# Fewer unread products that keep TensorE's clock up, and a norm root moved from GpSimd to VectorE, in a four-layer hybrid model

## The chip, the cores and the metric

The kernel runs on one core of a Trainium2 chip. Five engines work side by side on a core: TensorE (PE in the profile, its weight loads PEld), VectorE (DVE), ScalarE (ACT), GpSimd (POOL) and SyncE (SP), which only issues transfers here. Each engine takes its instructions in the order in which the program gives them, and they wait for each other by semaphores. The metric is the device time of one execution in microseconds (us); the time of a kernel is the median of its runs.

## The reference, cut to what matters

The model has four layers over 512 tokens of 1024 features, all in float32. Each layer is a token mixer of another kind and a SwiGLU network with 2816 hidden features; all have a root-mean-square norm ahead of them.

```python
for i in range(DEPTH):                       # 4 layers
    hn = rmsnorm(h, norm_mix[i])
    m = (rwkv7_mix, swa_sink_mix, sgu_chunk_mix, gla_mix)[i](hn, ...)
    h = h + m
    h = h + swiglu(rmsnorm(h, norm_ffn[i]), ffn_w_in[i], ffn_w_out[i])
return rmsnorm(h, norm_final)
```

The change touches the first mixer. It has 16 heads of 64 features. For every token a 64x64 state of each head is decayed, corrected and read; the read rows are then normed head by head, and it is the root of that norm which the change moves:

```python
def step(state, inp):
    r_t, d_t, k_t, v_t, kk_t, a_t = inp
    sa = jnp.einsum('bhvk,bhk->bhv', state, kk_t)
    state = (state * d_t[:, :, None, :]
             - sa[..., None] * (kk_t * a_t)[:, :, None, :]
             + v_t[..., None] * k_t[:, :, None, :])
    return state, jnp.einsum('bhvk,bhk->bhv', state, r_t)
...
mean = jnp.mean(y, -1, keepdims=True)
var = jnp.mean(jnp.square(y - mean), -1, keepdims=True)
y = ((y - mean) * lax.rsqrt(var + RW_GN_EPS)).reshape(B, S, D) * gn_g + gn_b
bonus = (jnp.sum(hs(r) * hs(k) * r_k, -1, keepdims=True) * hs(v)).reshape(B, S, D)
return ((y + bonus).astype(x.dtype) * g) @ w_o
```

## The kernel before, in words

**Products.** A float32 weight tile (`wraw`) arrives by a transfer. ScalarE rounds it to a high part (`whi`), VectorE takes the difference (`wlo`), and TensorE makes three products of high and low parts (`mm3`). Nearly all of TensorE's time goes to these. Plain float32 products, which go through TensorE in several passes and are seen as two records each in the trace, are used for small matrices and transposes.

**The first mixer.** Projections of r, k and v come first. The recurrence is then taken in chunks of 64 tokens, in four groups of four heads, n = 0 to 3. `ahead(n)` works out all of a group that needs no state: `rwkv_prepare` (decays by a scan, scaled keys), `rwkv_products` (64x64 products of the chunks, masked into `pr` or `pa`), `rwkv_inverse` (the inverse of a triangular 64x64 matrix for each chunk: blocks of 16 by 15 dependent pairs of a multiplication and a reduction on VectorE in `et`, then two levels of doubling in which products of 64x64 on TensorE alternate with steps on ScalarE and VectorE in `mt`; the results are `iv`) and `rwkv_direct`. `rwkv_chain(n)` walks through the eight chunks with the state (`st`); each step goes from TensorE to ScalarE (`vu`) and back, and to VectorE (`st`) and back. After every half of the chain `rwkv_out` norms the rows (`out`), adds the bonus and gates them into `rk`. `ahead(n + 1)` is written ahead of `rwkv_chain(n)`, so the two can be mixed. For n = 0 the tiles of the inverse are called `slot`, and the projection of v is mixed in. Then `rwkv_out_proj` multiplies by the output weights (`et,rk`), the last two rows of weights follow as `whi,rk`, and the rest of the model follows.

**The order of the work.** All calls on engines are recorded as operations with their dependencies (`record`, L234 calls each later, so that this line stands for nearly all instructions in the profile). `price` gives each a cost by engine, operation and width. `run` then walks through the recorded operations like a list scheduler: at each step it takes the operation that can start first by its own clock of the engines, and emits it. So the order on every engine follows from the costs.

**Unread products.** `run` also keeps an account of TensorE's columns: `count` notes when each product runs and how many columns it streams, scaled by the rows in use. Two functions put in products of the identity with itself, which nobody reads (`product`, L478, `ps<-ident` in the profile). `keep_warm` fills the time in which TensorE waits for more than 450 ns by the account. `ahead_of_cold` puts a single one in front of an operation if fewer than `DENSE` columns ran in the last `TICK` (3.41 us). Each takes a bank of PSUM of its own from the pool of eight, and so may wait until the last reader of that bank is done. In the account TensorE runs at half speed in any tick after one with fewer than `BUSY` columns.

**The norm root.** `rwkv_out` sums the 64 values of each of 8 heads on VectorE (`gmean`, `gvar`). The scaling by 1/64, the addition of epsilon and three Newton steps of the inverse root (`rsqrt8`) are done on GpSimd in operations of 128x8, the first guess on VectorE. A second version, `rsqrt`, which works on VectorE alone with one guess and nine operations, is used elsewhere in the kernel.

## Time and profile before

| | |
|---|---|
| median of three runs | 2604.63 us (2602.24 to 2613.82) |
| the profiled execution | 2609.04 us, span 2607.3 us |
| mean granted clock of TensorE | 0.995 |
| PE busy | 2551.3 us, 98% of the span |
| DVE, ACT, POOL busy | 1795.0, 1313.8 and 368.2 us |
| L478, unread products | 524 records (262 products), 84.6 us busy |
| the first mixer's recurrence | about 189 to 520 us of the span |

A busy PE is not a PE that does useful work: the unread products count as busy. A group's row gives busy time and mean duration, then the idle time of its engine ahead of it and who ended it. A row of the windows view gives the stretch, its length, and for each engine the busy time and number of records inside it, then PEclk, the clock that was granted to TensorE (1.00 is full speed, 0.50 half), the share of the transfer engines that was busy, and GB/s. A row of the timeline gives start, length, engine, line, operation, tiles, shape and number of merged records, and in brackets an idle time ahead of it with its releaser.

### The profile page before, as it was taken

To read this page: it belongs to the slowest core of one execution; us is meant where nothing else is said; L and a number is where in the kernel's file an instruction comes from. 1 tells how busy PE (TensorE), PEld (TensorE's weight loads), DVE (VectorE), ACT (ScalarE), POOL (GpSimd) and SP (SyncE) were. 2 spreads that over 40 slices of the span, in tenths; PEclk is the share of its full clock that TensorE was granted. 3 is DMA by queue.
4 is the path that set the end of the run, shared out by engine and by line. 5 is a ranking of instruction groups with operands and counts; after the bars stand their busy time and mean duration, and the time that the engine had idled before them with its cause. 6 is when DMAs were issued, how large, how long until landed. Compare 5 with 4: busy or idle time off the path is not lost.

```text
span 2607.3 us, 37842 instructions
## 1 busy us (share of the span) xinstructions
PE 2551.3 (98%) x14518; PEld 2077.8 (80%) x14518; DVE 1795.0 (69%) x2801; ACT 1313.8 (50%) x2161; POOL 368.2 (14%) x517
## 2 busy tenths in 40 slices
PE   9999999999999999999999999999999999999998
PEld 8577777997878766978887888898877777888786
DVE  7675756478778864787777555487868634577868
ACT  4534453375546555655464333465555523565555
POOL 0000111112121332121211000022111000121111
PEclk9999999999999999999999999999999999999999
DMA  5210001378898432788995332399997221499985
GB/s 168 68 60 10 10 4 58 102 160 214 216 220 207 106 96 49 158 213 220 218 231 146 97 90 85 80 217 229 209 213 181 89 81 57 97 220 224 219 199 116
DMA packets 126581, 367.32 MB, mean 141 GB/s; under 512 B 13360, under 2 KB 20016, under 8 KB 126400
## 3 DMA queue, kind: packets, MB, share of 16 engines
q0 software_dynamic: 41472, 138.43, 29.8%
q1 hardware_dynamic: 84928, 226.47, 26.8%
q8 instruction: 114, 1.87, 0.3%
q14 instruction: 67, 0.55, 0.1%
HBM read 360.39 MB, written 2.10 MB: 139 GB/s over the span
## 4 chain that ended last, share of the span: by engine, by line
PE 49%; DMA 5%; DVE 4%; issue 4%; ACT 3%; POOL 1%; SPq 0%; DVEq 0%; POOLq 0%; ACTq 0%
PE ps L234 49%; DMA wraw<-ffn_w_b 2%; DVE slot L234 2%; DMA wraw<-ffn_o_a 2%; ACT slot L234 1%; DVE wlo L234 1%; ACT whi L234 1%; POOL wraw L234 1%; DMA wraw<-ffn_w_a 0%; DVE h L234 0%; DVE mx L234 0%; PE ps L478 0%; DMA wraw<-sg_w_v 0%; DMA slot<-slot 0%; DVE left L234 0%
## 5 line engine op out<-in xcount | busy, mean ns | idle before, releaser
L234 PE MATMUL ps<-whi,slot 128*128 128x512 f32 (+1 forms) x5072 | 1557.5, 384 | 17.6 <-DVE h L234 7.9
L234 PEld LDWEIGHTS ps<-whi,slot 128*128 128x128 f32 x5072 | 941.9, 188 | 201.2 <-issue 21.9
L234 DVE TENSOR_TENSOR wlo<-wraw,whi 128x1024 fp32r<-128x1024 f32 (+2 forms) x632 | 726.3, 1155 | 403.9 <-ACT whi L234 401.5
L234 ACT CAST whi<-wraw 128x1024 fp32r<-128x1024 f32 (+3 forms) x632 | 625.4, 993 | 731.3 <-PE ps L234 554.8
L234 PE MATMUL ps<-wlo,slot 128*128 128x512 f32 (+1 forms) x2536 | 967.5, 382 | 1.3 <-DVE wlo L234 1.2
L234 PEld LDWEIGHTS ps<-wlo,slot 128*128 128x128 f32 x2536 | 476.1, 188 | 85.5 <-DVE wlo L234 5.0
L234 PE MATMUL ps<-slot,whi 128*128 128x512 f32 (+2 forms) x864 | 275.1, 396 | 0.4 <-DVE slot L234 0.3
L234 DVE TENSOR_TENSOR slot<-ps,slot 128x512 f32<-128x512 f32 (+2 forms) x287 | 154.9, 566 | 68.5 <-PE ps L234 50.7
L234 PEld LDWEIGHTS ps<-slot,whi 128*128 128x128 f32 (+2 forms) x864 | 156.9, 184 | 49.0 <-DVE slot L234 6.9
L234 POOL DMA_DIRECT2D wraw<-ffn_w_a x128 | 109.4, 855 | 511.5 <-DVE wlo L234 399.6
L234 PE MATMUL ps<-slot,wlo 128*128 128x512 f32 (+2 forms) x432 | 169.5, 393 | 0.0
L234 POOL DMA_DIRECT2D wraw<-ffn_w_b x64 | 54.8, 865 | 766.3 <-DMA wraw<-ffn_w_b 494.1
L234 DVE TENSOR_TENSOR slot<-left,slot 128x512 fp32r<-128x512 f32 (+1 forms) x214 | 137.7, 662 | 34.8 <-ACT slot L234 29.3
L234 DVE TENSOR_TENSOR h<-h,ps 128x512 f32<-128x512 f32 x192 | 127.2, 683 | 30.4 <-PE ps L234 28.9
L234 ACT CAST slot<-left 128x512 fp32r<-128x512 f32 (+1 forms) x214 | 123.8, 599 | 32.9 <-PE ps L234 26.4
L234 ACT COPY slot<-ps 128x512 f32<-128x512 f32 (+1 forms) x138 | 75.7, 565 | 59.6 <-PE ps L234 53.3
L234 PEld LDWEIGHTS ps<-slot,wlo 128*128 128x128 f32 (+2 forms) x432 | 79.5, 184 | 20.2 <-issue 3.3
L234 POOL DMA_DIRECT2D wraw<-ffn_o_a x64 | 54.6, 854 | 275.8 <-DVE wlo L234 161.3
L234 PEld LDWEIGHTS ps<-ident,slot 128*128 128x128 f32 (+2 forms) x672 | 67.9, 139 | 29.3 <-issue 8.3
L234 PE MATMUL ps<-ident,slot 128*128 128x128 f32 (+2 forms) x672 | 87.4, 264 | 1.9 <-DVE slot L234 1.7
L478 PE MATMUL ps<-ident 128*128 128x128 f32 x524 | 84.6, 297 | 4.0 <-POOL ident L234 1.4
L478 PEld LDWEIGHTS ps<-ident 128*128 128x128 f32 x524 | 71.6, 200 | 13.9 <-PE ps L478 5.7
(279 smaller groups left out, 2272.7 us busy)
## 6 DMA issues: line engine op xcount, KB each, us to landing
wraw<-ffn_w_a SPq DMA_DIRECT2D x128, 512.0 KB, 6.5
wraw<-ffn_w_a POOLq DMA_DIRECT2D x128, 512.0 KB, 6.2
wraw<-ffn_o_a SPq DMA_DIRECT2D x64, 512.0 KB, 5.1
wraw<-ffn_o_a POOLq DMA_DIRECT2D x64, 512.0 KB, 8.3
wraw<-ffn_w_b SPq DMA_DIRECT2D x64, 384.0 KB, 3.2
wraw<-ffn_w_b POOLq DMA_DIRECT2D x64, 384.0 KB, 6.3
wraw<-ffn_o_b SPq DMA_DIRECT2D x16, 512.0 KB, 4.4
wraw<-ffn_o_b POOLq DMA_DIRECT2D x16, 512.0 KB, 7.9
```

The lines of the kernel that those rows point to most:

```text
L234: op = self.add(eng.name, lambda: getattr(eng.target, what)(*map(real, args), **{k: real(a) for k, a in kw.items()}), *self.price(eng.name ...
L478: self.nc.tensor.target.matmul(self.ps.tile_pool.tile([P, S], F32, name="ps")[:, :P], self.ident.real(), self.ident.real(), start=True, st ...
```

## The change

Five things are edited.

1. The targets: `DENSE` goes from 3500 to 3000 columns a tick, `BUSY` from 3350 to 3000. `keep_warm` also stops as soon as more than `RICH` = 4200 columns ran in the tick that ends with the wait.
2. All unread products of one wait are put into one tile of PSUM. `ahead_of_cold` may put in up to four at once, as many as the target lacks.
3. `rsqrt8` goes. `rwkv_out` scales and adds epsilon on VectorE and calls `rsqrt`. The four constant tiles and their memsets on GpSimd go too.
4. Four charges in the planner's costs: VectorE operations that write a state tile (`st...`) cost 90 ns more, those of 32 rows 270 ns more, GpSimd operations at least 150 ns, and an unread product is charged with the turn of TensorE's form (92 ns) where the form changes.
5. As the costs set the order, the whole mixer is ordered anew. From the network of the first layer on, the order on TensorE is the same but for the unread products that are left out.

```diff
-    TICK, BUSY, DENSE = 10240 / 3, 3350.0, 3500.0
+    TICK, BUSY, DENSE, RICH = 10240 / 3, 3000.0, 3000.0, 4200.0
...
-            return 63.0 + n * (0.52 if fast else 2.1 if what == "tensor_tensor_scan" else 1.05) + 61.0 * columns, 250.0
+            slow = 90.0 if views[0].buf.name.startswith("st") else 270.0 if views[0].shape[0] == 32 else 0.0
+            return slow + 63.0 + n * (0.52 if fast else 2.1 if what == "tensor_tensor_scan" else 1.05) + 61.0 * columns, 250.0
...
-        return 37.0 + n * (0.83 if len(views) < 3 else 2.8 if views[0].dims[-1][0] < 32 else 2.4), 250.0
+        return max(150.0, 37.0 + n * (0.83 if len(views) < 3 else 2.8 if views[0].dims[-1][0] < 32 else 2.4)), 250.0
...
-        t = max(now, min(free) + self.SEM)
+        t, n = max(now, min(free) + self.SEM), 0
         while True:
-            c = 224.0 if work.get(int(t // self.TICK) - 1, 0.0) >= self.BUSY else 448.0
-            if t + c > s - self.TAIL:
-                return now
-            call()
-            self.fills += 1
+            c = 224.0 + (self.TURN if self.form[:2] != (P, P) else 0.0)
+            if work.get(int(t // self.TICK) - 1, 0.0) < self.BUSY:
+                c *= 2
+            if t + c > s - self.TAIL or self.armed and self.past(s) > self.RICH:
+                break
+            n += 1
             self.form = P, P, 0
             self.count(work, self.TICK, t, c, 512.0)
             t += c
             now = t
+        if n:
+            call(n)
+            self.fills += n
+        return now
...
-        cost = 224.0 if work.get(int(t // self.TICK) - 1, 0.0) >= self.BUSY else 448.0
-        call()
-        self.fills += 1
-        self.form = P, P, 0
-        self.count(work, self.TICK, t, cost, 512.0)
-        now["PE"] = t + cost
+        n = min(4, math.ceil((self.DENSE - sum_) / 280.0))
+        for _ in range(n):
+            cost = 224.0 + (self.TURN if self.form[:2] != (P, P) else 0.0)
+            if work.get(int(t // self.TICK) - 1, 0.0) < self.BUSY:
+                cost *= 2
+            self.form = P, P, 0
+            self.count(work, self.TICK, t, cost, 512.0)
+            t += cost
+        call(n)
+        self.fills += n
+        now["PE"] = t
         return True
+
+    def past(self, end):
+
+        sum_ = 0.0
+        for b, e, c in reversed(self.recent):
+            if e <= end - self.TICK:
+                break
+            sum_ += c * (e - max(b, end - self.TICK)) / (e - b)
+        return sum_
...
-        def product():
-            self.nc.tensor.target.matmul(self.ps.tile_pool.tile([P, S], F32, name="ps")[:, :P], self.ident.real(), self.ident.real(), start=True, stop=True)
-        self.nc.warm = self.ps, product, self.nc.ops[-1]
+        def products(n):
+            t, i = self.ps.tile_pool.tile([P, S], F32, name="ps")[:, :P], self.ident.real()
+            for _ in range(n):
+                self.nc.tensor.target.matmul(t, i, i, start=True, stop=True)
+        self.nc.warm = self.ps, products, self.nc.ops[-1]
...
-        nc.gpsimd.tensor_mul(mean, mean, self.k8['mean'])
+        nc.vector.tensor_scalar(mean, mean, 1.0 / 64, None, op0=ALU.mult)
...
-        nc.gpsimd.tensor_mul(var, var, self.k8['mean'])
-        nc.gpsimd.tensor_add(var, var, self.k8['eps'])
-        self.rsqrt8(rs, var)
+        nc.vector.tensor_scalar(var, var, 1.0 / 64, 64e-5, op0=ALU.mult, op1=ALU.add)
+        self.rsqrt(rs, var)
```

`rsqrt`, which is called instead, is this:

```python
nc.vector.tensor_scalar(y.bitcast(I32), x.bitcast(I32), -0.5, float(0x5f3759df), op0=ALU.mult, op1=ALU.add)
for _ in range(3):
    nc.vector.tensor_mul(t, y, y)
    nc.vector.scalar_tensor_tensor(t, x, -0.5, t, op0=ALU.mult, op1=ALU.mult)
    nc.vector.scalar_tensor_tensor(y, t, 1.5, y, op0=ALU.add, op1=ALU.mult)
```

By the order of the two programs, TensorE's unread products go from 262 in 74 blocks to 141 in 32. VectorE has 88 instructions more, eleven in each of the eight calls of `rwkv_out`; GpSimd has 128 operations of 128x8 and four memsets less; ScalarE has 26 table loads where it had 24.

On TensorE, in the inverse of group 0, which is mixed with the projection of v (`whi,slot` and `wlo,slot`; `slot,pa` are the inverse's products), the unread products stand like this; rows with - are of the kernel before, rows with + of the change:

```order
-L234 MATMUL ps<-slot,pa 64x64
-L478 MATMUL ps<-ident 128x128 x3
-L234 MATMUL ps<-slot,pa 64x64 x15
-L234 MATMUL ps<-wlo,slot 128x512
-L234 MATMUL ps<-whi,slot 128x512 x2
-L234 MATMUL ps<-wlo,slot 128x512
+L234 MATMUL ps<-slot,pa 64x64 x6
+L496 MATMUL ps<-ident 128x128
+L234 MATMUL ps<-slot,pa 64x64 x10
```

A run of sixteen 64x64 products is cut by one unread product where it was cut by three.

On TensorE again, at the start of the doubling of the inverse of group 3 (`ident,mt` is its first step, `ident,qk` and `v,pr` belong to group 3's direct terms and chain, `vu,pa` and `tg,g` to group 2), the kernel before has

```order
L234 MATMUL ps<-vu,pa 64x64 x4
L234 MATMUL ps<-tg,g_3946 128x256 x2
L478 MATMUL ps<-ident 128x128 x20
L234 MATMUL ps<-ident,mt 64x64 x16
L234 MATMUL ps<-ident,qk 128x128
L234 MATMUL ps<-mt,pr 64x64 x16
L234 MATMUL ps<-ident,qk 128x128 x3
L478 MATMUL ps<-ident 128x128 x2
L234 MATMUL ps<-mt 64x64 x16
```

and the change has

```order
L234 MATMUL ps<-v_2013,pr 64x64 x8
L234 MATMUL ps<-ident,qk 128x128 x4
L234 MATMUL ps<-v_2024,pr 64x64 x8
L496 MATMUL ps<-ident 128x128 x5
L234 MATMUL ps<-ident,mt 64x64 x16
L234 MATMUL ps<-st_1320,ident 128x128
L234 MATMUL ps<-mt,pr 64x64 x16
L234 MATMUL ps<-st_1320,ident 128x128
L234 MATMUL ps<-st_1320,h 128x128 x2
L234 MATMUL ps<-mt 64x64 x16
```

The twenty unread products ahead of the inverse are five, and between its steps stand steps of the chain of group 2 (`st...`), which in the kernel before was through by then.

On VectorE, in the inverse of group 1 (`et`), the norm root of group 0 (`gvar`, `grs`, `rs_t`) now stands between its dependent pairs; of the root's own operations only the guess `grs<-gvar` stood there before. The change has

```order
L234 TENSOR_SCALAR gvar<-gvar 128x8
L234 TENSOR_TENSOR et<-et 128x18
L234 TENSOR_SCALAR grs_2477<-gvar 128x8
L234 TENSOR_REDUCE et<-et 128x2x3
L234 TENSOR_TENSOR rs_t<-grs_2477 128x8
L234 TENSOR_TENSOR et<-et 128x32
L234 SCALAR_TENSOR_TENSOR rs_t<-gvar,rs_t 128x8
L234 TENSOR_REDUCE et<-et 128x2x4
L234 SCALAR_TENSOR_TENSOR grs_2477<-rs_t,grs_2477 128x8
```

where each operation of the root has one of the inverse ahead of it and behind it.

20 lines of the change are left out of this document (1 added, 19 removed).

## The prediction

> **What bounds the kernel now.** I read the page first: which engine is full, what the chain of work that ended last is made of, and what the unread products (L478) take.
>
> ```profile
> PE 2551.3 (98%) x14518; PEld 2077.8 (80%) x14518; DVE 1795.0 (69%) x2801; ACT 1313.8 (50%) x2161; POOL 368.2 (14%) x517
> PE 49%; DMA 5%; DVE 4%; issue 4%; ACT 3%; POOL 1%; SPq 0%; DVEq 0%; POOLq 0%; ACTq 0%
> L478 PE MATMUL ps<-ident 128*128 128x128 f32 x524 | 84.6, 297 | 4.0 <-POOL ident L234 1.4 <-DVE slot L234 1.3
> ```
>
> TensorE is full, so time is won by taking work from it or from its waits; but 84.6 us of its busy time are read by nobody. Next the windows view of L478 alone, with the borders of the mixer's stages: the inverse of group 0 (to 222), then the chains of groups 0, 1 and 2 (to 321, 376 and 458), group 3 (to 513), the wait for the last weights, and the rest.
>
> ```profile
> 189.00:222.00 33.00, 3.38 (x16) 2.23 (x16) 1.00 0.04 10
> 222.00:321.00 99.00, 17.55 (x116) 14.82 (x116) 0.97 0.03 10
> 321.00:376.00 55.00, 4.62 (x20) 2.90 (x20) 1.00 0.01 4
> 376.00:458.00 82.00, 19.92 (x118) 15.28 (x118) 1.00 0.14 47
> 458.00:513.00 55.00, 0.00 (x1) 0.00 (x0) 1.00 0.36 106
> 513.00:520.00 7.00, 5.42 (x46) 5.37 (x46) 1.00 0.37 108
> 1000.00:2607.00 1607.00, 5.96 (x32) 5.80 (x32) 1.00 0.66 159
> ```
>
> Two records are one product. Between 189 and 520 us they take 50.9 us in 46 blocks (the first and the last long one are shown below); after 1000 us only 6.0 us are left. The same stretches with all work:
>
> ```profile
> 222.00:321.00 99.00, 93.42 (x1139) 75.13 (x1137) 72.66 (x145) 47.95 (x96) 13.24 (x38) 0.97 0.03 10
> 376.00:458.00 82.00, 77.90 (x1037) 64.85 (x1035) 52.01 (x112) 32.60 (x75) 10.56 (x38) 1.00 0.14 47
> 458.00:513.00 55.00, 54.75 (x479) 51.75 (x479) 24.23 (x54) 18.45 (x40) 8.66 (x34) 1.00 0.36 106
> ```
>
> Without unread products TensorE works 75.9 of 99 us and 58.0 of 82 us in the chains of groups 0 and 2, while in group 3 it is full of real work. So the first two are bound by the steps between TensorE, VectorE and ScalarE. There are two kinds of blocks. The first delays what stands behind it:
>
> ```profile
> 191.16 0.98 PE L234 MATMUL ps<-ident,slot 64*64 64x64 f32 x28
> 192.07 0.49 PE L478 MATMUL ps<-ident 128*128 128x128 f32 x2
> 192.49 1.15 PE L234 MATMUL ps<-slot 64*64 64x64 f32 x32
> ```
>
> Fourteen 64x64 products (28 records) start within 0.91 us, 0.065 us each; one unread product among them puts the next 0.42 us off, so it costs 0.36 us. The second kind fills a wait:
>
> ```profile
> 418.19 1.13 PE L234 MATMUL ps<-tg,g 128*128 128x256 f32 x4
> 419.15 4.63 PE L478 MATMUL ps<-ident 128*128 128x128 f32 x40
> 423.75 1.15 PE L234 MATMUL ps<-ident,mt 64*64 64x64 f32 x32
> ```
>
> Twenty products in 4.60 us, 0.23 us each, until VectorE hands over the inverse. Going through the 46 blocks, I call a block delaying for the part in which the next product has its inputs already. That is 19.4 us: 2.9 up to 222, then 4.7, 3.0 and 5.6 by stage, and 3.1 at 513.
>
> **Part 1, fewer unread products.** By the order of the changed program the five stages with such products keep 3, 38, 5, 8 and 18, where they had 8, 58, 10, 59 and 23. At each stage's own price, the removed ones took 2.1, 6.0, 2.3, 17.2 and 1.2 us. What a removed product is worth depends on its kind. In the inverse of group 0 and the chain of group 1 nearly all delay: 2.1 and 2.0 us. At 513 a wait for weights is overrun, and five fewer give 1.1:
>
> ```profile
> 513.81 5.07 PE L478 MATMUL ps<-ident 128*128 128x128 f32 x44
> 518.63 1.18 PE L234 MATMUL ps<-whi,rk 128*128 128x512 f32 x4
> ```
>
> In the chain of group 2 delaying is 5.6 of 19.9; 51 of 59 products go, so 4.8 us are won outright and 12.4 us stood in waits. A wait doesn't go with its filler, but here the order moves: steps of group 2's chain now stand between the steps of group 3's inverse, and the preparation of group 3 begins during the inverse of group 2. Bounds: nothing of the 12.4, or all. I take half, 6.2, as VectorE is busy 52.0 of the stage's 82 us and so could feed a stage half-way between that and its length. In the chain of group 0 twenty products (6.0 us) go, and 38 stay, so its waits stay by the planner's own reckoning: half again, 3.0, bounds nothing and 6.0. One bank for a whole wait only spares an unread product the wait for a reader; that is within the delaying part. Sum of part 1: 2.1 + 3.0 + 2.0 + 11.0 + 1.1 = 19.2 us.
>
> **Part 2, the root on VectorE.** The root's last value comes late once in the chain of group 0, and the clock falls there:
>
> ```profile
> L234 POOL TENSOR_TENSOR rs<-rs,gvar x24: 202/203/712, 259.3 to 488.4; 128x8 f32<-128x8 f32 x24
> 279.54 0.65 POOL L234 TENSOR_TENSOR gvar<-gvar,k8half 128x8 f32<-128x8 f32 x1 [0.28 <-DVE grs L234]
> 285.11 1.08 DVE L234 TENSOR_TENSOR out<-out,grs 128x512 f32<-128x512 f32 x1 [1.78 <-POOL grs L234]
> 286.33 0.30 PE L234 MATMUL ps<-ident,out 128*128 128x128 f32 x1 [1.84 <-DVE out L234]
> 283.78:287.19 3.41, 1.36 (x15) 0.49 (x15) 2.08 (x3) 0.00 (x0) 3.10 (x8) 1.00 0.20 69
> 287.19:290.60 3.41, 3.41 (x43) 2.74 (x41) 3.41 (x5) 1.77 (x4) 1.31 (x3) 0.50 0.02 5
> 290.60:294.02 3.42, 3.42 (x40) 2.96 (x38) 1.70 (x4) 0.87 (x2) 0.00 (x0) 0.50 0.01 2
> ```
>
> GpSimd's thirteen operations take from 279.54 to VectorE's 285.11, 5.6 us; TensorE's queue stands behind a transpose of that value for 1.84 us and then runs 6.83 us at half speed, up to 3.4 us lost. On VectorE the same root takes less:
>
> ```profile
> 11.80 0.16 DVE L234 TENSOR_SCALAR rcol<-ms 128x4 int32<-128x4 int32 x1
> 11.99 0.16 DVE L234 TENSOR_TENSOR rs_t<-rcol 128x4 f32<-128x4 f32 x1
> 13.37 0.16 DVE L234 SCALAR_TENSOR_TENSOR rs_t<-ms,rs_t 128x4 f32<-128x4 f32 x1
> 258.57 0.16 DVE L234 TENSOR_TENSOR et<-et 128x2 f32<-128x2 f32 x1
> 258.65 0.17 DVE L234 TENSOR_SCALAR grs<-gvar 128x8 int32<-128x8 int32 x1
> 258.76 0.16 DVE L234 TENSOR_REDUCE et<-et 128x2 f32<-128x2 f32 x1
> ```
>
> From 11.80 to 13.37 eight steps, 0.196 us each, so ten take 2.0 us, 3.6 less than on GpSimd. The stall of 1.84 goes, and with it the fall of the clock, less a fifth for the chance that the wait shows elsewhere: 1.8 + 2.7 = 4.5 us; bounds nothing and 5.2. VectorE pays: 88 instructions. Between two dependent operations of the inverse there is room: 258.57 to 258.76 is 0.19 us with the guess in between, as long as one step alone. Interleaved like that they cost nothing; alone 11 x 0.196 = 2.2 us for each of eight calls. VectorE sets the pace during the inverses of groups 1 and 3, three or four calls, most of them interleaved: I take one call's price, 2.0 us, bounds 0 and 8.6 (four calls). The rest is covered by VectorE's idle time, 26 and 30 us in the two chains. GpSimd's queue holds little else there, so nobody gains from its 128 operations being gone.
>
> **Part 3, what it may cost.** Two more table loads on ScalarE:
>
> ```profile
> L234 ACT ACT_TABLE_LOAD x24 | 30.8, 1283 | 1.2 <-PEq L1849 0.8
> ```
>
> 2.6 us on an engine that is busy 48 of 99 us; I take 0.5. The clock is the larger unknown, as the target falls by a seventh. It is granted window by window of 3.41 us:
>
> ```profile
> 150.66:154.07 3.41, 1.68 (x11) 1.07 (x9) 3.37 (x7) 1.79 (x3) 0.00 (x0) 1.00 0.43 154
> 154.07:157.48 3.41, 3.35 (x14) 1.45 (x13) 3.37 (x9) 0.89 (x2) 0.00 (x0) 0.50 0.00 0
> 256.47:259.88 3.41, 2.49 (x32) 1.93 (x29) 3.23 (x12) 0.91 (x3) 1.18 (x6) 1.00 0.00 0
> 747.99:751.40 3.41, 1.65 (x9) 1.25 (x8) 3.01 (x4) 1.47 (x2) 0.00 (x0) 1.00 1.01 344
> ```
>
> A busy time of 1.68 us was too little at 150.66, and half speed followed; 2.49 us at 256.47, with no unread product in it, was enough; at 747.99 it was 1.65 us of full-width products, one of them unread, and the clock held. A cold window costs at most 1.7 us. The four network stages with a wait like that at 748 lose their unread product, and the recurrence runs nearer the edge; I take 2.5 us, bounds 0 and 7 (the four) outside the rival below. The Trainium skill, page "TensorE: Matmul & The Clock Gate", section "Why this matters for your kernels", asks only that no idle gap between bursts of products exceed about 3 us; by that the clock would cost nothing here, and the gain would be 21.5 us in place of 19.0. This trace disagrees with it: the window at 150.66 was half busy and the clock fell all the same.
>
> **The sum**: 19.2 + 4.5 - 2.0 - 0.5 - 2.5 = 18.7, and 0.3 for a block at 990 us that goes: 19.0 us. The profiled execution took 2609.04 us (its span 2607.3 and 1.7 around it) and becomes 2590.0. It lies 4.41 above the median of the three runs; taken from that median, 2604.63 - 19.0 = **2585.6 us**.
>
> **The rivals.**
>
> *The waits stay.* What the fillers of chains 0 and 2 hid is idle instead: 9.2 us less, 2594.8. For it: an unread product in a wait costs nothing, so taking it away gives nothing. Against it: the order really puts chain steps there.
>
> *All waits are filled.* The other half too, and costs near nothing: 19.0 + 9.2 + 4 = 32, 2572. For it: VectorE is idle 30 of 82 us in the chain of group 2. Against it: 38 products are still wanted in chain 0.
>
> *VectorE becomes the bound.* All 88 instructions on the path, 17.2 us instead of 2.0: 2600.8. Against it: 72.7 of 99 us busy, and the interleaving.
>
> *Slower: the clock falls in the recurrence.* Windows that the account puts just over 3000 columns are really under what the clock needs, as real waits are longer than planned ones. Each cold window loses 1.7 us; from the twelfth on (12 x 1.7 = 20.4) the gain is gone. There are 97 windows between 189 and 520 us; if one in four falls, 24 x 1.7 = 41, 2626. Against it: with the old target only one wait, at 283.78, led to cold windows in that part.
>
> That the change doesn't do what it says is excluded by the order: the unread products are gone from it.
>
> **How the numbers follow.** About 0.5%, 13 us, is what a measurement of this kernel tells from no change: faster is under 2591.6. Chances: forecast 0.50, waits stay 0.23, all filled 0.14, VectorE 0.05, clock 0.08. The forecast itself lies under 2591.6 nine times in ten (0.45), all filled always (0.14), waits stay three times in ten (0.07): faster 0.66, slower 0.08, the same 0.26. Range: 2570 reaches past the all-filled case; 2603 takes in the waits that stay with VectorE's upper bound.
>
> **What would show it.** L478's successor should take about 22 us between 189 us and the start of the network, for 50.9. The mixer's end (`whi,rk`, now 518.63) should come about 19 us earlier, most of it between the inverses of groups 2 and 3, and the stall at 286 should be gone. I am wrong if idle time of TensorE ahead of `mt`, `st` or `vu` grows by more than 15 us, if PEclk shows more than four cold windows in the recurrence, or if the gain arises after 520 us.

## The result and the profile after

The changed kernel takes 2571.07 us (median of 4 runs, 2563.79 to 2574.29); the kernel before, on the same chip, 2604.76 (4 runs, 2602.24 to 2613.82). The ratio is 0.9861, 95% interval [0.9829, 0.9892]. So it is faster, as forecast, but by some 34 us where 19.0 were worked out: the time lies by the rival "all waits are filled" (2572), not by the forecast (2585.6). Timed a second time beside the kernel before, the ratio was 0.9866 [0.9844, 0.9887].

The page of the changed kernel, its busy times and the engines in its chain of waits:

```profile
PE 2507.8 (98%) x14276; PEld 2039.3 (79%) x14276; DVE 1802.9 (70%) x2889; ACT 1317.5 (51%) x2163; POOL 337.5 (13%) x385
PE 49%; DMA 5%; DVE 4%; issue 4%; ACT 3%; POOL 0%; SPq 0%; DVEq 0%; POOLq 0%; ACTq 0%
```

TensorE is as full as before and has 43.5 us less to do (2551.3 before); VectorE has the 88 instructions of the root more and GpSimd 132 fewer. The unread products alone (their line is now 496), in stretches of the changed kernel's own times (columns: stretch, length, TensorE busy and records, weight loads, granted clock, DMA):

```profile
190.00:222.00 32.00, 1.47 (x6) 0.89 (x6) 1.00 0.04 10
222.00:321.00 99.00, 11.95 (x76) 9.78 (x76) 1.00 0.03 10
321.00:376.00 55.00, 1.54 (x10) 1.32 (x10) 1.00 0.02 4
376.00:458.00 82.00, 2.75 (x16) 2.09 (x16) 1.00 0.17 56
484.00:492.00 8.00, 4.34 (x36) 4.25 (x36) 1.00 0.67 161
880.00:960.00 80.00, 2.32 (x16) 1.94 (x16) 1.00 0.27 83
960.00:2569.00 1609.00, 0.00 (x0) 0.00 (x0) 1.00 0.64 159
```

The first five rows sum to 22.05 us: the "about 22 us" that the prediction asked for. The end of the mixer is read from the first product with the last weights (`whi,rk`, before at 518.63):

```profile
484.41 3.96 PE L496 MATMUL ps<-ident 128*128 128x128 f32 x34
488.12 0.71 PE L234 MATMUL ps<-whi,rk 128*128 128x512 f32 x2
```

It comes 30.5 us earlier, where 19 were expected. The windows view of all work shows in which stage. The borders are the first 64x64 `ident,mt` product of the inverses of groups 1, 2 and 3, and the last `et,rk` product ahead of the last weights (513.7 before, 484.3 after). First the kernel before (columns: stretch, length, busy time and records of TensorE, weight loads, VectorE, ScalarE and GpSimd, clock, DMA share, GB/s):

```profile
278.70:338.40 59.70, 55.82 (x800) 45.27 (x800) 44.03 (x92) 20.59 (x48) 8.86 (x20) 0.94 0.02 6
338.40:423.70 85.30, 83.25 (x1066) 67.71 (x1066) 57.66 (x124) 40.30 (x87) 14.56 (x56) 1.00 0.11 38
423.70:513.70 90.00, 87.29 (x1069) 78.59 (x1069) 36.93 (x73) 27.74 (x60) 13.03 (x50) 1.00 0.25 74
```

and the changed one:

```profile
276.50:331.70 55.20, 53.20 (x822) 43.20 (x822) 45.05 (x108) 23.86 (x53) 0.31 (x1) 1.00 0.02 7
331.70:396.60 64.90, 62.65 (x917) 49.94 (x917) 53.54 (x132) 35.15 (x72) 3.55 (x6) 1.00 0.08 28
396.60:484.30 87.70, 85.27 (x1084) 78.53 (x1085) 47.76 (x128) 34.48 (x75) 3.08 (x4) 1.00 0.27 87
```

Between the inverses of groups 2 and 3, 20.4 us are gone (85.3 to 64.9). VectorE was idle 27.6 us there and is now idle 11.4. In the last stage VectorE does 10.8 us more (36.93 to 47.76) and the stage is 2.3 us shorter all the same: VectorE had over 50 us to spare there. Steps of group 2's chain have moved from a stage that waits for VectorE into one that doesn't.

As work has crossed the border between them, these two stages have to be read together. Some 12 us of TensorE's real work left the first (busy time less unread products is 72.2 us before and 60.0 after) and went into the second, where 13.49 us of unread products had stood. Together the two are 22.7 us shorter (175.3 to 152.6); their unread products take 3.6 us for 24.5, and TensorE is idle 4.7 us for 4.8. So the time of the unread products is gone, and no wait has come in its place. Those of the first stage, before and after:

```profile
338.40:423.70 85.30, 11.05 (x74) 9.25 (x74) 1.00 0.11 38
331.70:396.60 64.90, 2.61 (x19) 2.30 (x18) 1.00 0.08 28
```

The other 6.9 us of the span (2607.3 to 2569.9 is 37.4) arise after the mixer. Measured at the same products, 5.9 us come between 868 and 1000 us of the kernel before, where two blocks of unread products of the attention layer stand; the gains and losses elsewhere sum to 1.0. The first block, in the kernel before, TensorE's products and then its weight loads:

```profile
918.13 3.05 PE L478 MATMUL ps<-ident 128*128 128x128 f32 x8 [0.66 <-DVE slot L234]
918.68 0.50 PEld L478 LDWEIGHTS ps<-ident 128*128 128x128 f32 x2 [0.25 <-PE ps L478]
919.53 0.50 PEld L478 LDWEIGHTS ps<-ident 128*128 128x128 f32 x2 [0.35 <-PE ps L478]
920.39 0.50 PEld L478 LDWEIGHTS ps<-ident 128*128 128x128 f32 x2 [0.35 <-PE ps L478]
```

and after:

```profile
885.60 1.16 PE L496 MATMUL ps<-ident 128*128 128x128 f32 x8 [0.67 <-DVE slot L234]
885.59 0.97 PEld L496 LDWEIGHTS ps<-ident 128*128 128x128 f32 x8 [1.07 <-DVE slot L234]
```

Four products with a tile each took 2.98 us to the next real product (918.13 to 921.11), since each waited for the one before it ("<-PE ps L478"); four in one tile took 1.08 (885.60 to 886.68). The description of the kernel gives each a bank of its own, but only the tile is its own: in the program of the kernel before, these four tiles lie in one and the same bank, and the second to the fourth wait by a semaphore until the product before them is done. Where tiles that follow each other lie in different banks, as with the twenty products at 419.15, which go round four banks, the products start 0.22 us apart. On one bank they start 0.55 us apart at full clock (four at 977.78) and 0.86 at half. In the profile before, the clock then stood at half speed for 6.83 us from 918.66 and 3.41 us from 980.10; after, it did at neither place. Two cold windows (windows at half speed) came in return, where waits of the network had lost their unread product; the first, in the timeline and in the windows view:

```profile
1231.44 0.47 PE L234 MATMUL ps<-whi,slot 128*128 128x512 f32 x1 [3.02 <-DVE h L234]
```

```profile
1229.15:1232.56 3.41, 1.12 (x5) 0.98 (x6) 2.64 (x4) 1.30 (x2) 0.00 (x0) 1.00 0.88 279
1232.56:1235.97 3.41, 3.41 (x10) 2.63 (x9) 1.22 (x1) 0.03 (x1) 0.00 (x0) 0.50 0.55 203
```

The wait at 1228.4 leaves a window with 1.12 us of work, and the next one runs at half speed; so again from 1860.61, after a wait of 1.99 us that left a window with 1.42 us of work.

### The profile page after: what moved, and what is told of

The parts are those of the page before. It is cut to its first block, busy times and chain, and to the rows that moved or that the text cites. A ratio compares the mean times of both kernels' runs of the same rounds, so it can differ in the third digit from the quotient of the medians.

```text
span 2569.9 us, 37305 instructions
## 1 busy us (share of the span) xinstructions
PE 2507.8 (98%) x14276; PEld 2039.3 (79%) x14276; DVE 1802.9 (70%) x2889; ACT 1317.5 (51%) x2163; POOL 337.5 (13%) x385
## 3 DMA queue, kind: packets, MB, share of 16 engines
q8 instruction: 112, 1.84, 0.3%
## 4 chain that ended last, share of the span: by engine, by line
PE 49%; DMA 5%; DVE 4%; issue 4%; ACT 3%; POOL 0%; SPq 0%; DVEq 0%; POOLq 0%; ACTq 0%
PE ps L234 49%; DMA wraw<-ffn_o_a 2%; DMA wraw<-ffn_w_b 2%; DVE slot L234 2%; ACT slot L234 1%; ACT whi L234 1%; DVE wlo L234 1%; DVE mx L234 1%; DVE h L234 0%; POOL wraw L234 0%; DMA wraw<-ffn_w_a 0%; DVE left L234 0%; DMA wraw<-sg_w_v 0%; DMA slot<-slot 0%; ACT left L234 0%
## 5 line engine op out<-in xcount | busy, mean ns | idle before, releaser
L234 PE MATMUL ps<-whi,slot 128*128 128x512 f32 (+1 forms) x5072 | 1557.5, 384 | 21.7 <-DVE h L234 10.6
L234 ACT COPY left<-ps 128x512 f32<-128x512 f32 x100 | 50.5, 555 | 54.1 <-PE ps L234 54.1
L234 DVE TENSOR_TENSOR slot<-slot 128x512 fp32r<-128x512 f32 (+9 forms) x93 | 61.2, 664 | 16.9 <-ACT slot L234 14.6
```

Of the source, the lines that this page charges most:

```text
L234: op = self.add(eng.name, lambda: getattr(eng.target, what)(*map(real, args), **{k: real(a) for k, a in kw.items()}), *self.price(eng.name ...
```

## The experiments

The first theory was that of the prediction: an unread product is worth what it delays, and moving the root is a small matter of its own. Its rival: what counts is which steps stand between which, and that is set by the root. Below, "the mixer's end" is the start of `whi,rk` in the profiled run (518.6 before, 488.1 after); gains in us are one less the ratio, times 2605 (36 for the change itself). "The two stages" are the one between the inverses of groups 2 and 3 and the one from there to the last `et,rk` product (175.3 us before, 152.6 after). What is said of places in the order, of banks and of counts of unread products is read from the programs.

### One part alone, or one part undone

**b_bank**: the kernel before, with one tile for unread products that follow each other.

```diff
-    ...matmul(self.ps.tile_pool.tile([P, S], F32, name="ps")[:, :P], ident, ident, ...)
+    if shared is None: shared = self.ps.tile_pool.tile([P, S], F32, name="ps")[:, :P]
+    ...matmul(shared, ident, ident, ...)   # shared is dropped at the next real instruction
```

> The kernel before, in its own order, with one edit: unread products that follow each other with no real product between share one PSUM tile. Theory 'own banks make the products of one wait wait for each other': the blocks of four ahead of the attention's products (3.0 and 2.1 us) shrink to about 1.1 us, the cold windows behind them go, 7 us there and 2 to 4 us in the recurrence: about 2594 us. Theory 'only the number of products and the order count': under 2 us, 2603 to 2606.

2595.49 us, ratio 0.9958 [0.9943, 0.9973], 11 us, as the first theory had it. The order of real work and the number of unread products are those of before; the mixer ends at 513.7, 4.9 us earlier, and the rest is gained behind it. In the kernel before, fifteen of the mixer's unread products lie on the bank of the one just ahead of them; at 0.55 us for 0.22 that makes about 4.9 us, by estimate, which is what came. The four products in the attention layer:

```profile
909.88 1.16 PE L485 MATMUL ps<-ident 128*128 128x128 f32 x8 [0.66 <-DVE slot L234]
910.97 3.19 PE L234 MATMUL ps<-slot 64*128 64x128 f32 x24
```

1.09 us instead of 2.98. (The second block of four takes 2.00 us in this profile, as it falls into a cold window.) The prediction had called this part "within the delaying part" and so priced it at nothing of its own.

**a_own**: the reverse, the changed kernel with a tile for each unread product.

```diff
-    t = ps tile; for _ in range(n): matmul(t, i, i)
+    for _ in range(n): matmul(ps tile, i, i)
```

> The changed kernel, in its own order, with one edit undone: every unread product takes a tile of its own again. Theory 'own banks': the two blocks in the attention grow back to 2 to 3 us with cold windows behind them, 7 to 10 us slower than the change, 2578 to 2581 us. Theory 'number and order': no more than 2 us slower, 2571 to 2573.

2577.13 us, 0.9881 [0.9862, 0.9899], a loss of 5 us, between the two theories and nearer to the first. The mixer's end is unmoved (487.0): of the products left there only one lies on the bank of the one just ahead. In the attention layer each of the two blocks of four lies on one bank again; the first takes 3.29 us (887.27 to 890.56), and the clock is at half speed there and behind (886, 948).

**b_root**: the kernel before with the norm's root on VectorE and nothing else.

```diff
-    nc.gpsimd.tensor_mul(mean, mean, self.k8['mean']) ... self.rsqrt8(rs, var)
+    nc.vector.tensor_scalar(mean, mean, 1.0 / 64, ...) ... self.rsqrt(rs, var)
```

> The kernel before with the norm root alone moved to VectorE (targets, banks and charges as before; the order follows from it). Theory 'the root is what lets the chain of group 2 overlap the inverse of group 3': 12 us or more of the 33 us appear, 2592 us or less. Theory 'the order comes from the charges and targets': only the stall at 286 us and the cold windows behind it go, 3 to 6 us, 2598 to 2602.

2594.65 us, 0.9953 [0.9936, 0.997], 12 us; the mixer's end is at 501.4, 17.2 us earlier. The prediction had 4.5 less 2.0 and 0.5 for the root. The stage between the inverses of groups 2 and 3:

```profile
333.60:402.00 68.40, 65.51 (x911) 52.19 (x911) 53.59 (x133) 35.44 (x70) 3.55 (x6) 1.00 0.03 5
```

68.4 us for 85.3, with the old targets and the old banks. So most of the 20.4 us of that stage come with the root. The last stage is 4.5 us longer (94.5 us), and the two stages together are 12.4 us shorter, of the change's 22.7. The unread products are 222 for 262, as the planner fits them to the order. Of the order, one thing changes much: the preparation of group 3 starts at the 1609th real product instead of the 1815th, and its inverse at the 2079th instead of the 2145th.

**a_root8**: the changed kernel with the root back on GpSimd.

```diff
-    self.rsqrt(rs, var)          # VectorE
+    self.rsqrt8(rs, var)         # GpSimd, with its constants k8
```

> The changed kernel with the root put back on GpSimd, all else as in the change. Theory 'the root': 12 us or more slower than the change, 2583 us or more. Theory 'charges and targets': 3 to 6 us slower, 2574 to 2577.

2587.58 us, 0.9927 [0.9904, 0.995]: 17 us of the change's gain are lost. The inverse of group 3 starts at 412.1 (396.6 in the changed kernel) and stands again at the 2145th product. In the profiled run, the fastest of the six, the mixer ends at 500.1, 12.0 us later, and the two stages take 165.0 us, 12.4 more. That is what b_root gives there, in the other direction.

**b_bankroot**: the kernel before with both, shared bank and root.

```diff
+    one tile for unread products that follow each other (b_bank)
+    root on VectorE (b_root)
```

> The kernel before with two of the edits, the shared bank and the root on VectorE; targets and charges as before. Alone they gave ratios of 0.9958 and 0.9953. Theory 'each works at a place of its own': they add, ratio 0.991, about 2582 us, and 11 us are left to targets and charges. Theory 'both spare the same waits': no more than the better one, 0.995, 2592 us.

2586.12 us, 0.9914 [0.9897, 0.9932], 22 us: 11 and 12 add.

**b_thr**: the kernel before with the two target numbers of the change.

```diff
-    TICK, BUSY, DENSE = 10240 / 3, 3350.0, 3500.0
+    TICK, BUSY, DENSE = 10240 / 3, 3000.0, 3000.0
```

> The kernel before with the two target numbers lowered to 3000 and nothing else: own banks, root on GpSimd, no new charges; 227 unread products in all, 126 of them in the mixer. Theory 'delays' (a removed product is worth its place on the path): some 145 fewer in the mixer, at 0.12 us each by the delaying share of the kernel before (19.4 us for 158 products), less the waits that stay, about 12 to 16 us: 2589 to 2593. Theory 'together' (the targets earn only where the root has moved and the products share a bank): 5 us or less, 2600 to 2605, as cold windows eat the rest.

2590.81 us, 0.9936 [0.9916, 0.9956], 17 us; the mixer's end is at 504.7, 13.9 us earlier. That is the time that "delays" forecast, but by luck: its sum took 145 products out of the mixer, and 32 went (157 to 125). The stage between the inverses of groups 2 and 3 is as long as before (329.2 to 414.7, 85.5 us), with 10.24 us at half speed, which can hide up to 5.1: the gain seen lies ahead of it and behind it.

**b_fill**: the kernel before with the whole new filling, the root still on GpSimd, no charges.

```diff
+    TICK, BUSY, DENSE, RICH = 10240 / 3, 3000.0, 3000.0, 4200.0
+    products(n): up to four at once, one tile for a wait
```

> The kernel before with the whole new filling (targets 3000 and 4200, up to four products at once, one bank for a wait), the root still on GpSimd, no new charges: 175 unread products. If the edits add, about 10 us from the bank and what the run with the targets alone gains: 2575 to 2585. If the targets need the root on VectorE, 2590 to 2596, with the last weights' first product at 500 us or later.

2593.2 us, 0.995 [0.9931, 0.9968], 13 us, mixer's end at 507.7. Time and end are those of the second expectation, but its reason doesn't hold: b_thr has 17 us without the root. The bank's 11 and the targets' 17 don't add here. The interval overlaps that of b_thr, and why the rest of the new filling adds nothing to the targets is left open. At the mixer's end, the 17.2 us of the root alone and the 10.9 of this run sum to 28.1, and the change has 30.5.

**a_oldthr**: the changed kernel with the old targets.

```diff
-    TICK, BUSY, DENSE, RICH = 10240 / 3, 3000.0, 3000.0, 4200.0
+    TICK, BUSY, DENSE, RICH = 10240 / 3, 3350.0, 3500.0, 1e9
```

> The changed kernel with the old targets (BUSY 3350, DENSE 3500, no RICH limit): 293 unread products instead of 141, 183 instead of 72 in the recurrence and the wait behind it; bank, root and charges as in the change. Theory 'the products delay': 8 us or more slower than the change, 2579 us or more. Theory 'they stand in waits': within 3 us, 2568 to 2574.

2604.77 us, 0.9986 [0.9974, 0.9998]: nearly all is lost, far more than the 17 us that the targets bring alone. With up to four products put in at once, the old targets lead to 293 unread products instead of 262, and the mixer's end goes to 519.8. The root is on VectorE here and the order is the early one (the preparation of group 3 from the 1609th product, its inverse at the 2087th), but 64 unread products stand between the inverses of groups 2 and 3, and that stage lasts 81.0 us. So the early order alone is not enough: the unread products must leave it the room. Putting in several at once needs the lower targets.

**a_nocharge**: the changed kernel without the four charges.

```diff
-    slow = 90.0 if ...("st") else 270.0 if views[0].shape[0] == 32 else 0.0
-    return max(150.0, ...)                                   # GpSimd
-    c = 224.0 + (self.TURN if self.form[:2] != (P, P) else 0.0)
+    c = 224.0
```

> The changed kernel with all four charges taken out of the planner's costs; bank, root and targets as in the change. Theory 'the charges make the planner let the chain of group 2 overlap the inverse of group 3': 8 us or more slower than the change, 2579 us or more, and a block of ten or more unread products is back ahead of that inverse. Theory 'root and targets do it': within 3 us of the change, 2568 to 2574.

2584.84 us, 0.9912 [0.9894, 0.993]. The mixer ends at 487.6 as in the changed kernel, so the charges bring nothing there, against the first theory. The loss of 13 us comes later: the attention layer's order is another one, and the profile shows half speed for 6.83 us at 887 and again at 958. Whether its order or those windows cost more was not separated.

### Leaving out the unread products

**b_nofill**: the kernel before in its own order; its unread products in the mixer are planned and then left out.

```diff
     def product():
+        if 600 < self.nc.pe_done < 2750: return
         ...
```

> The kernel before in its own order; its unread products between the start of the inverses and the wait for the last weights are planned, but left out of the program. Theory 'delays': the mixer ends up to 19 us earlier (whi,rk at about 500 us), less what cold windows cost; 2588 to 2595 if the clock holds. Theory 'order' (the time is set by which steps stand between which, and the fillers only fill): whi,rk at 514 us or later, 2600 to 2606.

2597.45 us, 0.9972 [0.9957, 0.9987], 7 us, between the two theories; the mixer's end is at 506.9, 11.7 us earlier, and TensorE stands at half speed for 34.1 us in six places on the way (from 239 to 447 us). The stage in question:

```profile
329.10:413.30 84.20, 73.65 (x994) 58.83 (x995) 57.73 (x124) 39.73 (x87) 14.64 (x56) 0.98 0.11 39
```

Without one unread product it lasts 84.2 us, 1.1 less than with 37 of them (3.4 us of it at half speed hide at most 1.7 more): TensorE is now idle for 10.6 us, for 2.0. So most of those products did fill waits, and taking them away gives next to nothing there. In the last stage (413.3 to 502.0) TensorE is idle for 7.0 us, for 2.7, and 20.4 us at half speed hide what else the products cost there. Over the two stages 12.8 us of waits come to light, and in the changed kernel they are filled with real work: it is idle for 4.7 us, with hardly an unread product.

**a_nofill**: the same with the changed kernel, without its 54 products in the mixer.

```diff
     def products(n):
+        if 600 < self.nc.pe_done < 2750: return
         ...
```

> The changed kernel in its own order, with the unread products of the recurrence (54 of the 141) planned but not put in; those at the start, ahead of the last weights and in the attention stay. Theory 'the change leaves no more than the clock needs': four or more cold windows in the recurrence, 1.7 us each, which outweigh some 6 us of delays: 2571 us or slower. Theory 'the target is still too high': at most one more cold window, 4 to 7 us faster than the change, 2564 to 2567.

2574.06 us, 0.9868 [0.9843, 0.9892], the mixer's end at 487.1. TensorE is idle 20.3 us in the mixer for 12.4, and it is cold for 23.9 us between 234 and 296: seven windows, as the first theory had it. What is left of unread products neither helps nor hurts.

**a_trim**: the changed kernel without the unread products that stand ahead of real work in the mixer, and with 9 for 17 ahead of the last weights.

```diff
-        call(n)                                       # ahead_of_cold
+        if not 600 < self.pe_done < 2750: call(n)
-    for _ in range(n): matmul(t, i, i)
+    for _ in range(9 if n == 17 else n): matmul(t, i, i)
```

> The changed kernel in its own order; the unread products that stand ahead of real work in the mixer are left out, and the block ahead of the last weights is cut from 17 products to 9. If they only delay: 5 us from the delays and 2 from the shorter block, 2564 to 2567. If they hold the clock: two or more cold windows come in the recurrence, and the time is 2571 or more.

2571.95 us, 0.9871 [0.9848, 0.9895]. The mixer ends at 481.1, 7 us earlier, as "they only delay" had it, though two cold windows stand in the recurrence (6.83 us from 234), and the end is the same: behind the mixer, cold windows at 712, 879, 1231 and 1859 (20.5 us in all, for 6.8 in the changed kernel's profile) can lose up to 6.8 us more.

### What the root's move really does

The root alone brought 17 us to the mixer's end. Two runs separate its time from its order.

**b_rootpos**: the kernel before in its own order on every engine; the sixteen small operations of each call run on VectorE where they stood for GpSimd.

```diff
-    op = self.add("POOL", lambda: nc.gpsimd.tensor_mul(...), price on POOL)
+    op = self.add("POOL", lambda: nc.vector.tensor_mul(...), price on POOL)   # the root only
```

> The kernel before in its own order on every engine as planned, with its own 262 unread products; only the root's sixteen small operations of each call run on VectorE where they stood on GpSimd. Theory 'time of the root' (each half's value comes some 3 us earlier and that is on the path): the last weights' first product at about 502 us for 518.6, 2588 to 2594. Theory 'order' (the move pays because the planner then prepares group 3 earlier): that product at 514 to 518 us, 2598 to 2605, with at most the stall at 286 us gone.

2608.72 us, 1.0009 [0.9997, 1.0022]: no gain, and slower than either theory had it. The operations do run on VectorE and faster (here one of the root's multiplications, 24 times at a median of 159 ns, for 201 on GpSimd), but the mixer's end is at 522.7. They are 128 more for VectorE, where the change has 88, so this is no exact price of the change's eleven. The durations (shortest, median, longest in ns), then the place of the old stall and the stage between the inverses:

```profile
L236 DVE TENSOR_TENSOR rs<-grs x24: 149/159/169, 257.9 to 492.8; 128x8 f32<-128x8 f32 x24
```

```profile
286.24 1.15 PE L236 MATMUL ps<-mt 64*64 64x64 f32 x32 [1.30 <-DVE rs L236]
288.05 1.02 PE L236 MATMUL ps<-et,sel 128*4 128x512 f32 x2 [0.67 <-DVE rs L236]
289.06 0.30 PE L236 MATMUL ps<-ident,out 128*128 128x128 f32 x1
```

```profile
338.90:428.20 89.30, 86.25 (x1066) 70.20 (x1067) 63.61 (x174) 40.15 (x87) 4.79 (x8) 0.96 0.11 36
```

The same products in the kernel before:

```profile
282.09 1.15 PE L234 MATMUL ps<-mt 64*64 64x64 f32 x32 [0.17 <-DVE mt L234]
283.48 1.02 PE L234 MATMUL ps<-et,sel 128*4 128x512 f32 x2 [0.24 <-DVE et L234]
```

The stall ahead of `ident,out` is gone as forecast (1.84 us at 286.33), but the two blocks ahead of it now wait for VectorE, which has the root in front: 1.30 and 0.67 us for 0.17 and 0.24. What the one wait gave back, the others took. The clock no longer falls at 287, but it falls for as long, 6.83 us, at 258.5. The stage between the inverses is 4 us longer, not shorter (it was cold for 6.83 us of it, which explains up to 3.4).

**b_win755**: the kernel before with the root on GpSimd; the planner considers the next 755 operations instead of 700.

```diff
-    WINDOW, SLACK, SEM = 700, 200.0, 100.0
+    WINDOW, SLACK, SEM = 755, 200.0, 100.0
```

> The kernel before with one number changed: the planner looks 755 operations ahead instead of 700. The root stays on GpSimd; the preparation of group 3 now begins at product 1609 of the real ones instead of 1815, as in the kernel with only the root moved, and its inverse at 2102 instead of 2145 (2079 there). Theory 'order': the mixer ends 10 to 17 us earlier, 501 to 508 us, 2588 to 2596. Theory 'time of the root': 514 us or later, 2600 to 2606.

2596.64 us, 0.9968 [0.9955, 0.9981], 8 us; the mixer's end is at 508.5, 10.1 us earlier, and the stage is 73.9 us long. Both lie just outside what "order" had, and far from the other:

```profile
335.90:409.80 73.90, 69.83 (x957) 55.72 (x956) 52.75 (x111) 35.96 (x73) 13.26 (x39) 0.98 0.08 26
```

With the root's work still on GpSimd (busy 13.26 us), 11 us of the stage go. The preparation of group 3 starts at the 1609th product here too. The planner also puts in fewer unread products (230 for 262, 18 for 37 in this stage), but b_nofill shows that leaving out all 37 in the old order brings 1.1 us there. So "order" holds and "time of the root" falls. The move of the root changes the list of operations that the planner orders (fewer of them, with other prices, on another engine), and it then prepares group 3 earlier. That is fragile: in orders that were planned and not timed, looking 745 or 760 ahead gives the early preparation too, 740 or 780 the late one. b_win755 doesn't reach the 17 us of b_root; its inverse of group 3 stands at the 2102nd product, not the 2079th, and whether that is the whole difference is not shown. Which of the planner's decisions turns first was not traced.

### Products for the network's waits

**a_guard**: the changed kernel, same order of real work; the 4200-column rule ends with the mixer, so 25 unread products come back later on.

```diff
-    ... or self.armed and self.past(s) > self.RICH:
+    ... or self.armed and self.pe_done < 2850 and self.past(s) > self.RICH:
```

> The changed kernel, same order of real work; the 4200-column rule ends where the mixer ends, so 24 unread products come back in waits of the network and the later layers. If the cold windows there cost what the clock shows: none at 1233 and 1861, and 3 us less, 2567 to 2569. If the products delay as much as they save: 2570 to 2573. If they overrun their waits: 2574 or more.

2567.46 us, 0.985 [0.9832, 0.9868]: inside the first range, but its interval overlaps those of the changed kernel (0.9861 and 0.9866), so no gain is shown. The wait at 1232 has its product again (0.38 us in it), and the profile shows no cold window from 246 us to the tail:

```profile
1232.46 0.38 PE L498 MATMUL ps<-ident 128*128 128x128 f32 x2
1233.62 0.47 PE L234 MATMUL ps<-whi,slot 128*128 128x512 f32 x1 [0.78 <-DVE h L234]
```

**a_trimguard**: both, a_trim and a_guard.

```diff
+    the edits of a_trim and of a_guard
```

> The changed kernel with both: 22 products fewer in the mixer (as in the run that ended it at 481 us and lost the gain to cold windows later), 24 more in the network's waits. If cold windows took that gain and the products hold the clock: 2560 to 2566, and the mixer's end at 481. If the clock falls all the same or elsewhere: 2568 to 2573.

2567.07 us, 0.9848 [0.9834, 0.9861], between the two forecasts. The mixer's end is at 482.8 and the windows at 1231 and 1859 are warm, but there are others (418, 715, 941).

**after_again and a_trimguard2**: these are the changed kernel and a_trimguard, unaltered, beside each other on one chip.

```diff
 (no edit)
```

> The changed kernel unaltered, once more, as the measure for the version with both: 2569 to 2573 us if its first time holds on this chip; a profile with another set of cold windows would show how much of the difference to the version with both is chance.

> The version with both, unaltered, beside the changed kernel on one chip: if it is faster, 3 to 6 us under that one (2564 to 2568); if the two are the same, within 2 us of it.

2568.7 us, 0.9866 [0.9844, 0.9887], and 2567.34 us, 0.9859 [0.9838, 0.9879]: the same. In this profile the changed kernel has neither of the windows at 1233 and 1861 (the clock, third figure from the end, is 1.00 around both places), and its span is 2559.9 us for 2569.9:

```profile
1220.00:1240.00 20.00, 18.43 (x82) 14.78 (x81) 14.42 (x18) 7.53 (x8) 2.93 (x4) 1.00 0.85 208
1845.00:1865.00 20.00, 19.40 (x86) 15.59 (x85) 14.46 (x17) 7.61 (x8) 3.07 (x4) 1.00 0.88 212
```

The waits themselves were shorter: the one of 3.02 us is 1.57 us long here (to 1227.99), the one of 1.99 is 0.60 (to 1852.26). Which waits turn cold differs from run to run of one program; a difference of one or two such windows between two profiles proves nothing of an edit.

## Why the prediction was right or wrong

**What bounds the kernel: right.** TensorE stayed at 98% with less to do, the chains of groups 0 and 2 were what gave, and 30.5 of the span's 37.4 us were won before the last weights.

**Part 1, the chain of group 2: the step that failed.** Of the 12.4 us in waits, "I take half, 6.2", with 4.8 outright, 11.0 in all. Between the inverses of groups 2 and 3 alone 20.4 us came, and 22.7 with the stage behind, which takes in a part of group 1's 2.0. The reason given (chain steps between the steps of group 3's inverse, an earlier preparation) was the right mechanism, and the 12.4 were about right (b_nofill brings 12.8 us of waits to light), but the half was a guess: all of them were filled. VectorE was called busy enough to feed "a stage half-way", and it went to 53.5 of 64.9 us; the steps also went into the next stage, where it had over 50 us to spare, which the prediction did not count. The other 9.9 of the 22.7 us are products that delayed, more than the 4.8 and 2.0 taken for them; some 3.9 (by the estimate for b_bank, twelve products) are those that waited for each other on one bank. As the clock fell there in b_nofill, this split is an estimate.

**Part 1, elsewhere: right at both ends, too much in the chain of group 0.** The inverse of group 0 gave 1.9 us for 2.1, read at the 1000th real product. The block ahead of the last weights takes 3.7 us for 4.8, as the forecast's 1.1 says. From the 1000th product to the inverse of group 2, where 3.0 of the chain of group 0, the root's 4.5 and some of the 2.0 of group 1 were expected, 4.8 us came, less than forecast.

**Part 2, the root: priced by its own operations, which is not what it earns.** The forecast took a stall and a cold clock of 4.5, less 2.0 of VectorE and 0.5 of ScalarE. b_rootpos comes nearest to measuring that price, and finds no gain (1.0009): the stall went and VectorE's queue took the same time from the inverse. What the prediction left out is that the root's move is what reorders groups 2 and 3. It had put this reordering under part 1, where no edit was named for it. b_root shows 12 us of time and 17.2 at the mixer's end, a_root8 17 us of time and 12.0 at the mixer's end.

**One bank: missed.** "Within the delaying part" can stand for the mixer (4.9 us in b_bank). But what sharing a tile spares is not the wait for a reader: it is that of products which lie on one bank in tiles of their own and wait for one another, 0.86 us apart at 918; in one tile, four take 1.08 us. That was in the trace of before, in the weight-load rows quoted above, and the prediction priced nothing behind 520 us but 0.3 us for a block at 990 and the clock in the network's waits.

**Part 3, the clock: the size was right in the one profile.** 2.5 us were taken for the four network waits; two cold windows came, at most 1.7 us each. In a second profile neither came. The Trainium skill, page "TensorE: Matmul & The Clock Gate", section "Why this matters for your kernels", asks for no idle gap of more than about 3 us. The wait of 3.02 us at 1228.4 that turned cold and the one of 0.78 us at 1232.8 (a_guard) that didn't agree with it; the wait of 1.99 us ahead of 1859.28, which turned cold too, and the half-busy window at 150.66 do not.

**The rivals.** "The waits stay" is what happens when nothing but the fillers goes (b_nofill); "all waits are filled" is what the full change does in the chain of group 2. That its time (2572) is so near the measured one is partly luck: it fills the waits of group 0's chain too, where less came than forecast, and has none of the 6.9 us behind the mixer. They weren't two chances of one event: what decided was whether the order moves and the unread products leave it room (a_oldthr), and that it moves could be read from the order of the program (inverse of group 3 at the 2099th product, not the 2145th) without a time. VectorE did not become the bound, and the clock held in the recurrence.

## What to carry to other kernels

Taking away a product that fills a wait gives next to nothing (1.1 us of 85.3 here), so ask which real work will stand in the wait instead. Find the edit that puts it there by undoing one edit at a time and comparing the orders of the programs, before any of them is priced. Where a planner sets the order, moving a few small operations can be worth far more than the price of the operations: 2.0 us net were forecast for the root here, 12 came with it alone, and none with the old order. Change one of the planner's numbers and see whether the order stays. And see in which bank a tile lies: a tile of its own is not a bank of its own.

## What the runs showed that was not expected

- Unread products, 128x128, in tiles of their own that lay on one bank waited for one another, although nobody reads what they write: 0.55 us from one to the next at full clock (977.78), 0.86 at half (919.53 to 920.39). On different banks it was 0.22 us (419.15), and in one tile four took 1.08 us.
- Faster operations on a busier engine gave nothing: one of the root's took 159 ns for 201, and the run 1.0009 of the time.
- The same program had cold windows at 154, 1233 and 1861 in one profile and only at 882 in another (the tail aside), with spans of 2569.9 and 2559.9 us. Leaving still more unread products out brought cold windows elsewhere and no time: a_nofill and a_trim end where the changed kernel does.
